# Normalizing and rotating q and k of two token tiles at a time in a hybrid attention layer

## The chip, the cores and the metric

The kernel runs on one core of a Trainium2 chip. The metric is the device time of one launch in microseconds (us), lower is better; a figure is the median of several runs. Engines are named as the profile names them: PE is TensorE (PEld its weight loads), DVE VectorE, ACT ScalarE, POOL GpSimd, SP the engine that issues most DMAs.

## The reference, cut to what matters

One layer of an encoder, 1024 tokens by 1024 channels, float32. The change touches how q and k are made from the normalized input h:

```python
proj = h @ w_in[l]
qa, ka, va, qb, kb, vb, gates = jnp.split(proj, split_at, axis=-1)
qa = rms_norm(qa.reshape(b, s, NA_HEADS, HEAD_DIM), g_qa[l])        # 8 heads of 64, no rotation
ka = rms_norm(ka.reshape(b, s, NA_HEADS, HEAD_DIM), g_ka[l])
o_a = neighbourhood_attention(qa, ka, va, rpb[l])
qb = partial_rotary(rms_norm(qb.reshape(b, s, DIL_HEADS, HEAD_DIM), g_qb[l]), pos)   # 12 heads of 64
kb = partial_rotary(rms_norm(kb.reshape(b, s, DIL_HEADS, HEAD_DIM), g_kb[l]), pos)
# three groups of 4 heads, each with dilated_window_attention; then gates, output projection, SwiGLU FFN
```

`rms_norm` divides each head's 64 values by the root of their mean square plus 1e-6. `partial_rotary` turns the first 16 of the 64 values by an angle that depends on the token.

## The kernel before, in words

The heads are worked in ten units of two heads: units 0 to 5 are the dilated heads (kinds 0, 1 and 2, two units each), units 6 to 9 the neighbourhood heads (the fourth kind, `U.kind == 3`). A unit has eight token tiles of 128 tokens. One step of the main loop, n = 8u + t, multiplies token tile t of unit u: `proj_chunk` (L333) makes 24 matmuls of 384 columns (q, k and v of two heads) into a bank of PSUM with the tag `d`, of which there are two, so that tile t + 2 needs the bank of tile t. Every float32 product is three products of split parts.

After the eight chunks of a step, `proj_post` takes the bank. ACT squares q and k into `sq` (L351) and copies them into `qn` (L352, 128 x 256: two heads of q, two of k). DVE sums the squares (L354), and `rstd` makes 1/rms: a logarithm and an exponential on ACT (L140, L142), then one Newton step on DVE with four small operations of 128 x 4 (L141, L143, L144, L145). DVE multiplies `qn` by it (L356). For kinds 0 to 2 POOL then rotates with four operations (L363 to L366). ACT copies v out (L368 or L371).

Two steps later `qk_turns` (L403) turns `qn` on PE with one transposition for q and one for k of each tile, and `qk_parts` (L425 to L428) writes the split parts into the unit's q and k. Before step 58 (`PAIRED`) the turns are made in odd steps n, for the tiles of steps n - 3 and n - 2 together; in steps 8 and 9 the first four tiles of unit 0 are turned, in steps 11 and 13 its last four. From step 58 each step turns the one tile of step n - 2. Between chunk 4 and chunk 5 of a step stand the scores of an earlier unit, its products with v, the turns, and the transpositions of its probabilities, in that order on PE. Other work of these steps runs on the same engines: the conditioning row `acc` on DVE (L322), weight splits (ACT L129; the low part on DVE or POOL, L130), parts of later weights (`tp`, `w1m`).

The order on PE is written out by hand. The orders on DVE, ACT, POOL and SP in the main loop are made when the program is built, by a list scheduler with a timeline of its own; `proj_post` has a raised priority. Each of these queues runs in order. `qn` has seven buffers of 256 values, taken in turn: the first for a placeholder, the second for the table of cosines, then one for each token tile. Steps up to 81 project and turn; from step 80 the gate matmuls (L773) follow, then merge, output projection and the feed-forward part (L1353, L1418, L1588).

Of the kernel before, what the change touches and what calls it, by code (L numbers as in the profile page):

```python
# [10 lines left out]
F32 = mybir.dt.float32  # L11
F32R = mybir.dt.float32r
AF = mybir.ActivationFunctionType
ALU = mybir.AluOpType
# [7 lines left out]
EPS = 1e-6  # L22
# [19 lines left out]
PAIRED, RBT, COMB = 58, 5, 68  # L42
# [6 lines left out]
def hybrid_layer(ctx: ExitStack, tc: tile.TileContext, x, colp, wada1, wada2, bada2, wqkv, wg, wpa, wpb,  # L49
                 wo, w1, w2, hgain, ropeg, rope, rbias, bmask, g2r, out):  # L50
    nc = tc.nc
# [45 lines left out]
    eps = const.tile([128, 1], F32, name="eps")  # L97
    nc.vector.memset(eps, EPS)
    for i in (0, 2):
        nc.vector.scalar_tensor_tensor(hg[:, i:i + 1], hg[:, i:i + 1], 0.125, hg[:, i + 1:i + 2],  # L100
                                       op0=ALU.mult, op1=ALU.mult)
# [34 lines left out]
    def rstd(p, n, width, ss, tag):  # L136
        v = p.tile([128, width], F32, tag="rv", bufs=3, name="rv")
        y = p.tile([128, width], F32, tag="ry", bufs=3, name="ry")
        z = p.tile([128, width], F32, tag="rz", bufs=3, name="rz")
        nc.scalar.activation(y, ss, AF.Ln, scale=1.0 / n, bias=eps)  # L140
        nc.vector.tensor_scalar(v, ss, 1.0 / n, EPS, op0=ALU.mult, op1=ALU.add)  # L141
        nc.scalar.activation(y, y, AF.Exp, scale=-0.5)  # L142
        nc.vector.tensor_mul(z, y, v)  # L143
        nc.vector.scalar_tensor_tensor(z, z, -0.5, y, op0=ALU.mult, op1=ALU.mult)  # L144
        nc.vector.scalar_tensor_tensor(y, z, 1.5, y, op0=ALU.add, op1=ALU.mult)  # L145
        return y
# [7 lines left out]
    ap_ = pool("attn", "right")  # L154
# [9 lines left out]

    yT = [ap_.tile([128, 4, S], F32, tag="qk", bufs=2, name="yT") for _ in range(2)]
    land = [big("land") for _ in range(NLAND)]
    for tag, n, bufs in (("bm", 512, 1), ("p", 512, 4), ("qn", 256, 7), ("rtab", 512, 1), ("acc2", 512, 1), ("pT", 512, 4),
                         ("stg", 512, 3), ("vs", 128, 2), ("ra", 64, 2), ("rb", 64, 2)):
        ap_.tile([128, n], F32, tag=tag, bufs=bufs, name="place")
    seq = [0]  # L170

# [89 lines left out]
    rtab = []  # L261

    def rope_tab():
        cs = ap_.tile([128, 4, 64], F32, tag="qn", bufs=7, name="cs").rearrange("p h (a b) -> p (h a) b", b=32)
        nc.sync.dma_start(cs, rope)
        tb = ap_.tile([128, 8, 2, 2, 16], F32, tag="rtab", bufs=1, name="rtab")
        for qk in range(2):
            for f in range(2):
                nc.gpsimd.tensor_tensor(tb[:, :, f, qk, :], cs[:, :, f * 16:f * 16 + 16],
                                        rg[:, qk, f, None, :].to_broadcast([128, 8, 16]), op=ALU.mult)  # L270
        return tb

# [71 lines left out]
    @urgent(PP)  # L344
    def proj_post(U, t):
        pd = U.pd[t]
        qn = ap_.tile([128, 4, 64], F32, tag="qn", bufs=7, name="qn")
        U.qn[t] = qn
        pq = pd[:, :256].rearrange("p (h d) -> p h d", h=4)
        sq = ap_.tile([128, 256], F32, tag="sq", bufs=1, name="sq")  # L350
        nc.scalar.activation(sq, pd[:, :256], AF.Square)  # L351
        nc.scalar.activation(qn, pq, AF.Copy)  # L352
        ss = ap_.tile([128, 4], F32, tag="ss4", bufs=2, name="ss4")
        nc.vector.tensor_reduce(ss, sq.rearrange("p (h d) -> p h d", h=4), axis=mybir.AxisListType.X, op=ALU.add)  # L354
        r = rstd(ap_, 64, 4, ss, "q")
        nc.vector.tensor_tensor(qn, qn, r[:, :, None].to_broadcast([128, 4, 64]), op=ALU.mult)  # L356
        if U.kind < 3:
            ra = ap_.tile([128, 4, 16], F32, tag="ra", bufs=2, name="ra")
            rb = ap_.tile([128, 4, 16], F32, tag="rb", bufs=2, name="rb")
            tb = U.tab[:, t]  # L360
            v4 = lambda z: z.rearrange("p (a b) c -> p a b c", a=2)
            tv = lambda f, c0, c1: tb[:, f, :, None, c0:c1].to_broadcast([128, 2, 2, c1 - c0])
            nc.gpsimd.tensor_tensor(v4(ra), v4(qn[:, :, 0:16]), tv(0, 0, 16), op=ALU.mult)  # L363
            nc.gpsimd.tensor_tensor(v4(rb[:, :, 0:8]), v4(qn[:, :, 8:16]), tv(1, 0, 8), op=ALU.mult)
            nc.gpsimd.tensor_tensor(v4(rb[:, :, 8:16]), v4(qn[:, :, 0:8]), tv(1, 8, 16), op=ALU.mult)
            nc.gpsimd.tensor_tensor(qn[:, :, 0:16], ra, rb, op=ALU.add)  # L366
        if U.kind == 0:
            nc.scalar.activation(U.v[:, t, :], pd[:, 256:384], AF.Copy)  # L368
        else:
            vs = ap_.tile([128, 128], F32, tag="vs", bufs=2, name="vs")  # L370
            nc.scalar.activation(vs, pd[:, 256:384], AF.Copy)  # L371
            vd = v_d[U.u - 2]
            if U.kind == 3:
                nc.scalar.dma_start(vd.rearrange("(c r j) d -> r j c d", c=8, r=16)[2 * t:2 * t + 2], vs)
            else:
                nc.scalar.dma_start(vd[t * 128:(t + 1) * 128, :], vs)
            if t == 7:
                U.v = big("v", [128, 8, 128])
# [479 lines left out]
    units = []  # L858
# [147 lines left out]
    for n in range(6, 92):  # L1006
# [46 lines left out]

        turns = [(units[0], tt) for tt in {8: (0, 1), 9: (2, 3), 11: (4, 5), 13: (6, 7)}.get(n, ())]
        if PAIRED <= n <= 81 or 9 < n < PAIRED and n % 2:
            turns += [(units[m // 8], m % 8) for m in ((n - 2,) if n >= PAIRED else (n - 3, n - 2)) if m >= 8]
        chunk()
        chunk()
        if n == PAIRED - 1:
# [693 lines left out]
```

## Time and profile before

| | |
|---|---|
| median of 3 runs | 1496.59 us (1496.54 to 1497.46) |
| the profiled execution: its time / its span from first to last instruction | 1494.47 us / 1492.7 us |
| busy share: PE, DVE, ACT, POOL | 99%, 72%, 47%, 40% |
| mean granted TensorE clock | 0.998 of full speed |

Read the shares with care: matmuls are pipelined and their ends are modelled, so a busy PE is not PE at its peak. Idle time of an engine that is not the bottleneck costs nothing.

### The profile page before, as it was taken

How to read it: one execution, taken by the hardware profiler on the slowest of the kernel's cores; microseconds unless marked ns; L12 is line 12 of the kernel's file. 1: busy time of each engine (PE TensorE's matmuls, PEld its weight loads, DVE VectorE, ACT ScalarE, POOL GpSimd, SP SyncE). 2: the span in 40 equal slices, each digit the busy share in tenths (PEclk: the TensorE clock that was granted, in tenths of full speed). 3: DMA queues.
4: the chain of work that ended last, by engine and by line, in shares of the span. 5: the costliest groups of instructions: out<-in, count | busy, mean ns of one | idle time of the engine just before them, and what ended most of it. 6: DMA issues, size and time to landing. Idle time of an engine off the chain costs nothing. (4 is left out here: it accounts for less than half of the span.)

```text
span 1492.7 us, 24300 instructions
## 1 busy us (share of the span) xinstructions
PE 1473.4 (99%) x8168; PEld 1260.0 (84%) x8168; DVE 1074.1 (72%) x2202; ACT 700.4 (47%) x1775; POOL 591.9 (40%) x580
## 2 busy tenths in 40 slices
PE   9999999999999989999999999999999999999998
PEld 7999998989898867888888888888888888887886
DVE  6877767667768854485765596888777777598468
ACT  5655665556776655465422353323223333354442
POOL 0342342242100122256431402677777775204464
PEclk9999999999999999999999999999999999999999
DMA  9725454576144454773452335345533334898342
GB/s 357 263 73 166 155 164 146 181 243 204 56 138 136 154 198 150 265 291 116 133 192 85 99 92 184 123 144 167 177 106 106 109 107 151 282 369 280 99 155 99
DMA packets 156908, 250.54 MB, mean 168 GB/s; under 512 B 26832, under 2 KB 70512, under 8 KB 156016
## 3 DMA queue, kind: packets, MB, share of 16 engines
q1 hardware_dynamic: 138208, 235.35, 47.0%
q10 hardware_dynamic: 18576, 13.64, 2.8%
q8 instruction: 65, 1.06, 0.3%
q14 instruction: 59, 0.48, 0.1%
HBM read 184.06 MB, written 64.86 MB: 167 GB/s over the span
## 5 line engine op out<-in xcount | busy, mean ns | idle before, releaser
L333 PE MATMUL ps_d<-whi,hT 128*128 128x384 f32 x1152 | 310.2, 340 | 1.6 <-ACT vs L371 0.8
L129 ACT ACTIVATE whi<-raw 128x512 fp32r<-128x512 f32 (+2 forms) x314 | 182.6, 594 | 210.7 <-PE ps_t L1588 33.5
L130 POOL TENSOR_TENSOR wlo<-raw,whi 128x512 fp32r<-128x512 f32 (+2 forms) x123 | 159.9, 1307 | 288.2 <-ACT whi L129 251.9
L130 DVE TENSOR_TENSOR wlo<-raw,whi 128x512 fp32r<-128x512 f32 (+1 forms) x191 | 167.9, 894 | 62.3 <-ACT whi L129 57.0
L333 PEld LDWEIGHTS ps_d<-whi,hT 128*128 128x128 f32 x1152 | 209.2, 188 | 3.6 <-ACT vs L371 1.2
L333 PE MATMUL ps_d<-wlo,hT 128*128 128x384 f32 x576 | 193.0, 335 | 0.8 <-POOL wlo L130 0.6
L333 PEld LDWEIGHTS ps_d<-wlo,hT 128*128 128x128 f32 x576 | 108.4, 188 | 1.3 <-POOL wlo L130 1.3
L129 ACT ACTIVATE whi<-ws 128x512 fp32r<-128x512 f32 x60 | 37.7, 628 | 119.5 <-DVE ws L1435 85.2
L1368 POOL TENSOR_TENSOR e<-e,c 128x512 f32<-128x512 f32 x44 | 68.5, 1556 | 60.6 <-DVE c L1498 36.5
L773 PE MATMUL ps_d<-hT,whi 128*128 128x512 f32 x256 | 81.4, 399 | 3.4 <-ACT whi L129 3.4
L363 POOL TENSOR_TENSOR ra<-qn,rtab 128x64 f32<-128x64 f32 x48 | 17.6, 367 | 142.8 <-DVE qn L356 121.0
L130 POOL TENSOR_TENSOR wlo<-m,whi 128x512 fp32r<-128x512 f32 x35 | 51.9, 1493 | 53.6 <-ACT whi L129 53.6
L1366 ACT ACTIVATE e<-e 128x512 f32<-128x512 f32 x44 | 27.4, 630 | 89.2 <-DVE e L1501 60.7
L130 POOL TENSOR_TENSOR wlo<-gl,whi 128x512 fp32r<-128x512 f32 x26 | 35.4, 1377 | 73.2 <-ACT whi L129 73.2
L581 ACT ACTIVATE P<-P,st 128x256 f32<-128x256 f32 (+2 forms) x100 | 45.7, 458 | 34.1 <-DVE st L579 33.9
L1418 PE MATMUL ps_v<-h2T,whi 128*128 128x512 f32 x192 | 59.2, 390 | 0.0
L1418 PE MATMUL ps_s<-h2T,whi 128*128 128x512 f32 x192 | 59.1, 389 | 0.0
L773 PEld LDWEIGHTS ps_d<-hT,whi 128*128 128x128 f32 x256 | 47.9, 191 | 13.1 <-ACT whi L129 3.6
L1418 PE MATMUL ps_d<-h2T,whi 128*128 128x512 f32 x184 | 56.7, 390 | 0.0
L1367 DVE TENSOR_TENSOR e<-e 128x512 f32<-128x512 f32 x44 | 42.9, 981 | 17.9 <-ACT e L1366 17.8
L140 ACT ACTIVATE ry<-ss,eps 128x4 f32<-128x4 f32 (+1 forms) x88 | 26.2, 298 | 61.1 <-DVE ss L354 45.1
L517 ACT ACTIVATE P<-P,sx 128x384 f32<-128x384 f32 (+1 forms) x64 | 37.2, 582 | 34.3 <-DVE sx L516 34.1
(411 smaller groups left out, 4052.5 us busy)
## 6 DMA issues: line engine op xcount, KB each, us to landing
raw<-in_w_dram SPq DMA_DIRECT2D x139, 256.0 KB, 3.2
ga_d<-e SPq DMA_DIRECT2D x77, 256.0 KB, 2.0
raw<-ga_d SPq DMA_DIRECT2D x77, 256.0 KB, 2.6
wa<-in_wada_dram SPq DMA_DIRECT2D x32, 512.0 KB, 5.3
raw<-in_wqkv_dram SPq DMA_DIRECT2D x80, 192.0 KB, 4.9
m<-in_w_dram SPq DMA_DIRECT2D x44, 256.0 KB, 5.1
xt<-in_x_dram SPq DMA_DIRECT2D x16, 512.0 KB, 4.2
land<-in_wada_dram SPq DMA_DIRECT2D x16, 512.0 KB, 9.3
```

Of the source, the lines that this page charges most:

```text
L129: nc.scalar.activation(hi[:, :n], r, AF.Copy)
L130: (eng or nc.gpsimd).tensor_sub(lo[:, :n], r, fview(hi[:, :n]))
L140: nc.scalar.activation(y, ss, AF.Ln, scale=1.0 / n, bias=eps)
L333: nc.tensor.matmul(pd[:, :384], tok(a, k, t), U.w[k][b][:, :384], start=(k == 0 and i == 0), stop=(k == KT - 1 and i == 2))
L363: nc.gpsimd.tensor_tensor(v4(ra), v4(qn[:, :, 0:16]), tv(0, 0, 16), op=ALU.mult)
L517: nc.scalar.activation(P[:nq, :nk], P[:nq, :nk], AF.Exp, scale=-1.0, bias=nm, accum_out=sm)
L581: nc.scalar.activation(C.P[h][:nq, c], C.P[h][:nq, c], AF.Exp, scale=-1.0, bias=nm, accum_out=sm)
L773: nc.tensor.matmul(pb, w[x][:, k * 128:(k + 1) * 128], b[y][:, k], start=(k == 0 and q == 0), stop=(k == 3 and q == 2))
L1366: nc.scalar.activation(sg, a, AF.Sigmoid)
L1367: nc.vector.tensor_mul(sg, sg, a)
L1368: nc.gpsimd.tensor_mul(sg, sg, up)
L1418: nc.tensor.matmul(pb, w[p][:, k * 128:(k + 1) * 128], b[q][:, k], start=(k == 0 and i == 0), stop=(k == 3 and i == 2))
```

## The change

1. `qn` becomes a tile for two neighbouring token tiles (128 x 8 x 64; three buffers in place of seven of half that size). Each tile still has its own square, copy, sum and copy of v; the copy of v (`proj_v`) stands ahead of the rest.
2. After the odd tile, 1/rms, the multiplication and the rotation are made once for both tiles, at twice the width.
3. The Newton step has two DVE operations in place of four: the copy out of PSUM carries a factor -1/128, ACT squares the estimate, and the constants are folded.
4. The rotation table's axes are reordered to fit, and the small tiles `ra`, `rb` are twice as wide.
5. From step 58 a step turns the tile of step n - 3 in place of n - 2; at t = 1 it turns tiles 6 and 7 of the unit before together, at t = 2 none.

```diff
-                         ("stg", 512, 3), ("vs", 128, 2), ("ra", 64, 2), ("rb", 64, 2)):
+    ... ("qn", 512, 3) for ("qn", 256, 7)
+                         ("stg", 512, 3), ("vs", 128, 2), ("ra", 128, 2), ("rb", 128, 2)):
...
     def proj_post(U, t):
         pd = U.pd[t]
-        qn = ap_.tile([128, 4, 64], F32, tag="qn", bufs=7, name="qn")
-        U.qn[t] = qn
+        i = t % 2
+        if i == 0:
+            U.two = (ap_.tile([128, 8, 64], F32, tag="qn", bufs=3, name="qn"),
+                     ap_.tile([128, 8], F32, tag="ss4", bufs=2, name="ss4"))
+        qn, ss = U.two
+        hs = slice(4 * i, 4 * i + 4)
+        U.qn[t] = qn[:, hs]
...
-        nc.scalar.activation(qn, pq, AF.Copy)
-        ss = ap_.tile([128, 4], F32, tag="ss4", bufs=2, name="ss4")
-        nc.vector.tensor_reduce(ss, sq.rearrange("p (h d) -> p h d", h=4), axis=mybir.AxisListType.X, op=ALU.add)
-        r = rstd(ap_, 64, 4, ss, "q")
-        nc.vector.tensor_tensor(qn, qn, r[:, :, None].to_broadcast([128, 4, 64]), op=ALU.mult)
+        nc.scalar.activation(qn[:, hs], pq, AF.Copy, scale=-1.0 / 128)
+        nc.vector.tensor_reduce(ss[:, hs], sq.rearrange("p (h d) -> p h d", h=4), axis=mybir.AxisListType.X, op=ALU.add)
+        proj_v(U, t, pd)
+        if i == 0:
+            return
+        y, y2, z, r = (ap_.tile([128, 8], F32, tag=g, bufs=3, name=g) for g in ("rv", "ry", "rz", "rz"))
+        nc.scalar.activation(y, ss, AF.Ln, scale=1.0 / 64, bias=eps)
+        nc.scalar.activation(y, y, AF.Exp, scale=-0.5)
+        nc.scalar.activation(y2, y, AF.Square)
+        nc.vector.scalar_tensor_tensor(z, ss, 64 * EPS, y2, op0=ALU.add, op1=ALU.mult)
+        nc.vector.scalar_tensor_tensor(r, z, -192.0, y, op0=ALU.add, op1=ALU.mult)
+        nc.vector.tensor_tensor(qn, qn, r[:, :, None].to_broadcast([128, 8, 64]), op=ALU.mult)
         if U.kind < 3:
...
+            nc.gpsimd.tensor_tensor(...)  four rotation operations, each over [128, 8, 16] or [128, 8, 8]
...
-            turns += [(units[m // 8], m % 8) for m in ((n - 2,) if n >= PAIRED else (n - 3, n - 2)) if m >= 8]
+            turns += [(units[m // 8], m % 8) for m in ((n - 3, n - 2)[:(2, 0)[t - 1] if t in (1, 2) else 1] if n >= PAIRED else (n - 3, n - 2)) if m >= 8]
```

## Rows read from the trace of the kernel before

**Rows 1.** The page's first part: busy us, share of the span, instructions.
```profile
PE 1473.4 (99%) x8168; PEld 1260.0 (84%) x8168; DVE 1074.1 (72%) x2202; ACT 700.4 (47%) x1775; POOL 591.9 (40%) x580
```
**Rows 2.** Busy time by stretch: us, each engine's busy us (instructions), clock, DMA.
```profile
90.00:320.00 230.00, 225.92 (x1694) 211.20 (x1693) 163.76 (x542) 136.83 (x480) 73.42 (x174) 1.00 0.48 153
320.00:520.00 200.00, 199.16 (x1459) 179.12 (x1457) 154.01 (x526) 137.34 (x453) 29.88 (x25) 1.00 0.48 154
520.00:550.00 30.00, 25.55 (x149) 19.21 (x149) 16.96 (x39) 14.81 (x39) 9.12 (x7) 0.94 0.62 208
550.00:1300.00 750.00, 750.00 (x3436) 619.54 (x3435) 523.60 (x706) 282.46 (x528) 377.59 (x264) 1.00 0.45 152
```
**Rows 3.** PE's waits from 50 to 560: us in total, times, longest.
```profile
PE ps_v L403 <- POOL qn L366: 2.7, 3, 1.3
...
PE ps_d L333 <- ACT vs L371: 0.8, 1, 0.8
PE ps_d L333 <- ACT whi L129: 0.8, 1, 0.8
PE ps_d L333 <- POOL wlo L130: 0.6, 1, 0.6
```
**Rows 4.** DVE groups from 56 to 520, shapes apart: busy us, mean ns, idle before.
```profile
L356 DVE TENSOR_TENSOR qn<-qn,ry 128x256 f32<-128x256 f32 x80 | 36.6, 458 | 3.0
...
L143 DVE TENSOR_TENSOR rz<-ry,rv 128x4 f32<-128x4 f32 x80 | 25.8, 322 | 29.1 <-ACT ry L142 28.4
...
L141 DVE TENSOR_SCALAR rv<-ss 128x4 f32<-128x4 f32 x80 | 17.1, 214 | 1.5
L145 DVE SCALAR_TENSOR_TENSOR ry<-rz,ry 128x4 f32<-128x4 f32 x80 | 14.2, 178 | 1.3
...
L144 DVE SCALAR_TENSOR_TENSOR rz<-rz,ry 128x4 f32<-128x4 f32 x80 | 13.3, 166 | 1.8
...
L827 DVE TENSOR_TENSOR tp<-tp 128x512 f32<-128x512 f32 x8 | 5.6, 704 | 6.7 <-DMA tp<-h_d 6.6
```
**Rows 5.** ACT groups from 56 to 520, shapes apart.
```profile
L140 ACT ACTIVATE ry<-ss,eps 128x4 f32<-128x4 f32 x80 | 23.9, 298 | 59.8 <-DVE ss L354 45.1 <-DVE rv L141 8.0 <-DMA raw<-in_wqkv_dram 2.9
...
L142 ACT ACTIVATE ry<-ry 128x4 f32<-128x4 f32 x80 | 16.2, 203 | 1.7
```
**Rows 6.** POOL groups from 56 to 520, shapes apart.
```profile
L363 POOL TENSOR_TENSOR ra<-qn,rtab 128x64 f32<-128x64 f32 x48 | 17.6, 367 | 142.8 <-DVE qn L356 121.0 <-DVE rv L141 13.3 <-DVE rz L143 7.6
...
L364 POOL TENSOR_TENSOR rb<-qn,rtab 128x32 f32<-128x32 f32 x48 | 14.4, 300 | 0.0
```
**Rows 7.** PE at 143 to 145: start us, us, instruction, idle before.
```profile
144.31 0.44 PE L403 MATMUL ps_v<-ident,qn 128*128 128x128 f32 x2 [0.24 <-POOL qn L366]
```
**Rows 8.** PE at 189 to 197.
```profile
193.21 0.44 PE L403 MATMUL ps_v<-ident,qn 128*128 128x128 f32 x2 [1.16 <-POOL qn L366]
```
**Rows 9.** PE at 303 to 305.
```profile
304.24 0.44 PE L403 MATMUL ps_v<-ident,qn 128*128 128x128 f32 x2 [1.28 <-POOL qn L366]
```
**Rows 10.** PE at 276 to 279: four transpositions in one row.
```profile
277.81 0.83 PE L403 MATMUL ps_v<-ident,qn 128*128 128x128 f32 x4
```
**Rows 11.** PE at 130 to 133.
```profile
131.91 0.66 PE L403 MATMUL ps_v<-ident,qn 128*128 128x128 f32 x4
```
**Rows 12.** POOL at 185 to 194.
```profile
186.48 1.37 POOL L363 TENSOR_TENSOR ra<-qn,rtab 128x64 f32<-128x64 f32 x1 [7.54 <-DVE qn L356]
187.81 1.71 POOL L364 TENSOR_TENSOR rb<-qn,rtab 128x32 f32<-128x32 f32 x1
```
**Rows 13.** PE at 78 to 79, the end of step 9 and the start of step 10.
```profile
77.93 0.60 PE L403 MATMUL ps_s<-ident,qn 128*128 128x128 f32 x4
78.29 0.42 PE L333 MATMUL ps_d<-whi,hT 128*128 128x384 f32 x1
```
**Rows 14.** ACT at 73 to 75.
```profile
73.88 0.38 ACT L352 ACTIVATE qn<-ps_t 128x256 f32<-128x256 f32 x1
```

More of the change, by code (lines that the diff above doesn't have):

```diff
@@ L166, in hybrid_layer @@
     land = [big("land") for _ in range(NLAND)]
-    for tag, n, bufs in (("bm", 512, 1), ("p", 512, 4), ("qn", 256, 7), ("rtab", 512, 1), ("acc2", 512, 1), ("pT", 512, 4),
-                         ("stg", 512, 3), ("vs", 128, 2), ("ra", 64, 2), ("rb", 64, 2)):
+    for tag, n, bufs in (("bm", 512, 1), ("p", 512, 4), ("qn", 512, 3), ("rtab", 512, 1), ("acc2", 512, 1), ("pT", 512, 4),
+                         ("stg", 512, 3), ("vs", 128, 2), ("ra", 128, 2), ("rb", 128, 2)):
         ap_.tile([128, n], F32, tag=tag, bufs=bufs, name="place")
@@ L263, in rope_tab @@
     def rope_tab():
-        cs = ap_.tile([128, 4, 64], F32, tag="qn", bufs=7, name="cs").rearrange("p h (a b) -> p (h a) b", b=32)
+        cs = ap_.tile([128, 8, 64], F32, tag="qn", bufs=3, name="cs")[:, :4].rearrange("p h (a b) -> p (h a) b", b=32)
         nc.sync.dma_start(cs, rope)
-        tb = ap_.tile([128, 8, 2, 2, 16], F32, tag="rtab", bufs=1, name="rtab")
+        tb = ap_.tile([128, 2, 8, 2, 16], F32, tag="rtab", bufs=1, name="rtab")
         for qk in range(2):
             for f in range(2):
-                nc.gpsimd.tensor_tensor(tb[:, :, f, qk, :], cs[:, :, f * 16:f * 16 + 16],
+                nc.gpsimd.tensor_tensor(tb[:, f, :, qk, :], cs[:, :, f * 16:f * 16 + 16],
                                         rg[:, qk, f, None, :].to_broadcast([128, 8, 16]), op=ALU.mult)
@@ L351, in proj_post @@
         nc.scalar.activation(sq, pd[:, :256], AF.Square)
-        nc.scalar.activation(qn, pq, AF.Copy)
-        ss = ap_.tile([128, 4], F32, tag="ss4", bufs=2, name="ss4")
-        nc.vector.tensor_reduce(ss, sq.rearrange("p (h d) -> p h d", h=4), axis=mybir.AxisListType.X, op=ALU.add)
-        r = rstd(ap_, 64, 4, ss, "q")
-        nc.vector.tensor_tensor(qn, qn, r[:, :, None].to_broadcast([128, 4, 64]), op=ALU.mult)
-        if U.kind < 3:
[L358 to L362, printed above, removed]
+        nc.scalar.activation(qn[:, hs], pq, AF.Copy, scale=-1.0 / 128)
[10 more added lines that the diff above has]
+        nc.vector.tensor_tensor(qn, qn, r[:, :, None].to_broadcast([128, 8, 64]), op=ALU.mult)
+        if U.kind < 3:
+            ra = ap_.tile([128, 8, 16], F32, tag="ra", bufs=2, name="ra")
+            rb = ap_.tile([128, 8, 16], F32, tag="rb", bufs=2, name="rb")
+            tb = U.tab[:, :, t - 1:t + 1].rearrange("p f t a c -> p f (t a) c")
+            v4 = lambda z: z.rearrange("p (a b) c -> p a b c", b=2)
+            tv = lambda f, c0, c1: tb[:, f, :, None, c0:c1].to_broadcast([128, 4, 2, c1 - c0])
             nc.gpsimd.tensor_tensor(v4(ra), v4(qn[:, :, 0:16]), tv(0, 0, 16), op=ALU.mult)
@@ L366, in proj_post, with proj_v @@
             nc.gpsimd.tensor_tensor(qn[:, :, 0:16], ra, rb, op=ALU.add)
+    def proj_v(U, t, pd):
         if U.kind == 0:
```

## The prediction

> **What bounds the kernel now.** I read the page's first part first, then busy time by stretch, then PE's waits, then the operations that the change touches, then single stretches of the timeline. The first part shows PE busy for 1473.4 of 1492.7 us [rows 1]; all its idle time is 19.3 us, and whatever the other engines save can only come out of that. The stretches show where it lies: 4.08 us between 90 and 320 (kinds 0 to 2), 0.84 between 320 and 520 (the fourth kind), 4.45 between 520 and 550, and none from 550 to 1300 [rows 2]. The rest lies in the start and the tail, which the change does not touch.
>
> PE's waits in the projection steps say what could be won: three waits at the turns, L403, for POOL's last rotation operation, 2.7 us together; one for a bank that ACT had not yet copied out, 0.8; one for a high weight part on ACT, 0.8; one for a low part on POOL, 0.6 [rows 3]. Together 4.9 us, a third of a per cent. A change of under 0.2%, 3 us, can hardly be told from none on this kernel. The idle time between 520 and 550 stands at the gates' weights, after the last unit; the change moves no load and no gate operation there, so I leave it.
>
> **The change part by part.** The sum is made on the profiled execution, 1494.47 us, with 1492.7 of span and 1.8 around it; it stands 2.1 under the median of the runs, 1496.59.
>
> *What DVE and ACT get rid of.* Each of 80 tiles costs DVE L141, L143, L144, L145 and L356, 0.214 + 0.322 + 0.166 + 0.178 + 0.458 = 1.338 us, 107 us in all [rows 4]. After the change each of 40 pairs has two small operations like L144 and L145 and one multiplication of 128 x 512. That one is not in the trace; the nearest row is L827, a two-operand operation of that size, 0.704 [rows 4]. So 40 x (0.166 + 0.178 + 0.704) = 42 us, 65 us less. ACT loses 80 x (0.298 + 0.203) = 40 us for the logarithm and the exponential and gets back half of it, and 40 squares of 128 x 8, which I bound by these two operations, 0.2 to 0.3 us [rows 5]: some 10 us less. None of this counts by itself: between 90 and 320 DVE is busy 163.76 of 230 us and PE 225.92 [rows 2], and PE's matmuls hide it. It counts where it shortens a queue that PE waits for.
>
> *The chain of the odd tile grows.* Until now the even tile was finished a step ahead; now the odd tile's chain does it for both. The multiplication grows by 0.704 - 0.458 = 0.25 us. On POOL an operation of 64 values takes 0.367 and one of 32 takes 0.300 [rows 6], two of each for a tile: 1.33 us. The slope is 0.067 for 32 values, so 128 values give about 0.50, and the pair 2 x (0.50 + 0.367) = 1.74, 0.40 more. (Bounds: no growth, and twice, 1.33 more.) The Newton step loses L143, 0.322, and gets the square, 0.2 to 0.3: nearly nothing. So the pair is ready 0.25 + 0.40 - 0.07 = about 0.58 us later after the same start in kinds 0 to 2, 0.2 in the fourth.
>
> *What this meets at the turns.* Before step 58 the turn comes in the second step after the odd tile's projection, before and after the change. Three turns already wait, at 144.31, 193.21 and 304.24 [rows 7 to 9], and one at 277.81 takes 0.83 us for its four transpositions, where an undisturbed one takes 0.66 [rows 10, 11]: it has no slack either. With the queues as they stand, these four end 4 x 0.58 = 2.3 us later, and at the three that wait the even tile's two transpositions, 0.22 each time by the pitch of the rows, no longer run ahead: 0.66. Together +3.0. The other end: DVE no longer works off the even tile's chain and one link less stands in the odd one's, so that less foreign work gets in between, and all 2.7 us of waiting go. The queue orders are made anew when the program is built, so the trace cannot say which; I take the middle, +0.1, and keep both ends.
>
> *The other waits.* The copy of v now stands ahead of 1/rms, and ACT, DVE and POOL have less to do. The bank wait and the two weight waits, 0.8 + 0.8 + 0.6 [rows 3], may go, all or none; as a new order can make others of their kind, I take off less than half, 0.9.
>
> *Three buffers for seven.* In steady state a `qn` tile is turned at least a step before its buffer is wanted again. Not at the start. The placeholder, the cosine table and the pairs take buffers in turn, so tiles 0 and 1 of unit 1 get the buffer of tiles 2 and 3 of unit 0, which are turned at the end of step 9. The copy of unit 1's tile 0, now made right after step 8, must wait for that, and it holds bank `d`, which the first matmul of step 10 wants. That matmul follows the four transpositions directly: they start at 77.93 and end at 78.53, the matmul starts at 78.29 [rows 13]. A copy takes 0.38 [rows 14], so the bank is free at 78.91 at the earliest: 0.62 us of new waiting, 1.0 if one more copy stands ahead. I take 0.7. Behind that copy ACT's queue holds this step's other copies, for which nobody waits before step 11.
>
> *The fourth kind a step later.* From a tile's being ready to its turn it is two steps now; it stays two for the even tiles and for 6 and 7, and becomes three for the other odd ones. Scores need all eight tiles, and tiles 6 and 7 are still turned at t = 1, one step ahead of the first scores. Three units lose one turn each, a handful of ACT and DVE operations under a PE that idles 0.84 us in that whole stretch [rows 2]. I count nothing; without that cover it would be 0.4 us per operation, on ACT or DVE alone. No DMA is added, and none of SP's moves past another.
>
> *Sum:* +0.1 - 0.9 + 0.7 = -0.1 us: 1494.4 for a profiled execution, 1496.5 for the median.
>
> **The rivals.** *Faster: the stalls go.* All 4.9 us of the projection steps' waits vanish and the bank wait of step 10 stays: -4.2, 1492.4. For it: DVE has 65 us less in stretches where it is busy seven tenths, and each of the waits was a queue that ran late, not a lack of throughput. Against it: the three longest end on POOL, whose chain grows.
>
> *Slower: rotation of the pair gets stretched by VectorE.* At 186.48 one rotation operation took 1.37 us and the next 1.71, four to six times their usual length, [rows 12] against [rows 6]. If POOL's two longer operations of the pair meet such a neighbour, the pair is late by more. It decides from 0.58 us at the four tight turns on, with nothing won back (+3.0 + 0.7). At 1.0 us: 4 x 1.0 + 0.66 + 0.7 = +5.4, 1502.0 without the relief, 1501.1 with it. For it: such stretches exist. Against it: their means, 0.367 and 0.300, hold them already.
> The Trainium skill, GPSIMD Engine Reference, section 8 (Key points), says that this engine shares its SBUF interfaces with VectorE and contends with VectorE instructions that have two SBUF inputs; the stretched rows agree with it, as such operations run beside them, and the pair's multiplication is one more of that sort, twice as long. By it the change would go against itself; the price is the one above.
>
> *The change does nothing at all for PE:* all waits stay as they are but for step 10's, +0.7, 1497.3. That is inside "no change" as well.
>
> **How the numbers follow.** No measurable change: 0.52, as the whole stake on either side is about 5 us and the terms have both signs. Faster by over 3 us: 0.24; nearly all of the waits must go. Slower by over 3 us: 0.24; the pair must be late at several turns. The likeliest case by itself reaches from 1493.6 to 1499.6. The range takes in all waits won, 1496.6 - 5.1, and a pair that is a microsecond late, 1501.5.
>
> **What would show it.** Right: PE's idle time between 90 and 320 stays at 2 to 6 us; the multiplication takes about 0.7 us and POOL's two wide operations about 0.5; PE waits 0.6 to 1.0 us for ACT near 78; DVE's busy time falls by some 65 us and the total does not follow. Wrong: turns that wait for POOL in most units, a new wait of the fourth kind's scores, or a changed stretch between 520 and 550, where the clock was 0.94 [rows 2] behind a stall; a stall that moves there would cost or give back more than its own length.

## The result and the profile after

The changed kernel takes 1503.38 us (median of 4 runs, 1502.5 to 1505.48), the kernel before 1496.70 beside it (1496.54 to 1497.46): 1.0045 times as long, 95% interval 1.003 to 1.006, or 6.7 us. The forecast said 1496.5 and 1491.5 to 1501.5. It is slower, beyond the range. The profiled execution took 1503.9, span 1502.1.

The page's first part of the changed kernel answers to [rows 1]:

```profile
PE 1475.9 (98%) x8168; PEld 1261.7 (84%) x8168; DVE 1029.0 (69%) x1916; ACT 693.6 (46%) x1729; POOL 573.3 (38%) x484
```

VectorE (DVE) works 45 us less (the times of its single operations, added up, fall by 61; the records overlap, and busy time counts an overlap once), ScalarE (ACT) 7, POOL 19; PE's idle time went from 19.3 to 26.2 us. Work was saved, and PE waits more. The stretches of the changed kernel answer to [rows 2]:

```profile
90.00:320.00 230.00, 225.52 (x1683) 211.37 (x1682) 144.32 (x410) 134.78 (x468) 56.13 (x100) 0.99 0.45 144
320.00:520.00 200.00, 196.56 (x1442) 178.65 (x1441) 133.83 (x404) 131.37 (x426) 31.97 (x27) 1.00 0.48 157
520.00:550.00 30.00, 25.23 (x154) 18.67 (x153) 17.74 (x45) 14.27 (x39) 2.58 (x2) 0.92 0.62 214
550.00:1300.00 750.00, 750.00 (x3441) 618.77 (x3440) 519.42 (x709) 284.85 (x535) 384.42 (x268) 1.00 0.45 149
```

From 90 to 320 PE idles 4.48 us (before 4.08), which looks like nothing; from 320 to 520 it idles 3.44 (before 0.84). PE's waits from 50 to 560 answer to [rows 3] (total, times, longest):

```profile
PE ps_d L787 <- ACT whi L129: 4.4, 1, 4.4
PE ps_v L417 <- POOL qn L378: 2.6, 4, 1.2
PE ps_d L333 <- POOL wlo L130: 2.1, 2, 1.4
PE ps_s L516 <- DVE qk L442: 1.8, 1, 1.8
PE ps_v L417 <- DVE qn L368: 1.3, 1, 1.3
PE ps_d L333 <- ACT whi L129: 1.3, 1, 1.3
PE ps_d L333 <- ACT v L382: 0.7, 1, 0.7
PE ps_s L516 <- ACT qk L440: 0.3, 1, 0.3
```

L787 stands at the gates and is no part of the change. The other lines sum to 10.1 us where [rows 3] had 4.9. New are the fourth kind's scores L516 (2.1), a turn that waits for VectorE's multiplication (1.3; at 332.62 in step 51, the first pair of unit 6, so a turn of the fourth kind, which has no rotation), a bank that waits for the copy of v (0.7, at step 10) and one more wait for a low weight part (1.4). The new operations on VectorE and POOL from 56 to 520 answer to [rows 4] and [rows 6]:

```profile
L368 DVE TENSOR_TENSOR qn<-qn,rz 128x512 f32<-128x512 f32 x39 | 27.0, 692 | 3.0 <-ACT qn L357 0.6 <-DVE rz L367 0.5
L366 DVE SCALAR_TENSOR_TENSOR rz<-ss,ry 128x8 f32<-128x8 f32 x39 | 10.0, 257 | 24.5 <-ACT ry L365 24.5
L367 DVE SCALAR_TENSOR_TENSOR rz<-rz,rv 128x8 f32<-128x8 f32 x39 | 8.2, 209 | 0.9
```

```profile
L378 POOL TENSOR_TENSOR qn<-ra,rb 128x128 f32<-128x128 f32 x24 | 12.7, 529 | 1.6
L375 POOL TENSOR_TENSOR ra<-qn,rtab 128x128 f32<-128x128 f32 x24 | 12.1, 505 | 156.8 <-DVE qn L368 116.1 <-ACT sq L356 13.1 <-DVE rz L367 11.5
L376 POOL TENSOR_TENSOR rb<-qn,rtab 128x64 f32<-128x64 f32 x24 | 10.2, 423 | 0.0
L377 POOL TENSOR_TENSOR rb<-qn,rtab 128x64 f32<-128x64 f32 x24 | 9.5, 398 | 0.0
```

A pair's rotation is 1.855 us long (forecast 1.74).

**Where the time went.** PE runs the same 8168 matmuls before and after, so the start of the k-th can be compared in the two traces. The difference grows by 9.4 us in all, since this profiled execution of before was a short one (1494.47). It grows by 1.3 before 56 us, where nothing was changed; executions differ by that much (`e2` below, as little changed there, is 0.8 ahead at 38 us). Then come 1.31 at 74.87 (low part), 0.92 at 81.8 (bank), 2.0 up to 269 (0.4 of it in the weights' wait that ends at 263.39, 1.6 behind it), 1.33 at 272.4 (turn), 1.33 at 332.6 (turn), 2.4 at 421.9 to 424.1 (scores), and 1.3 at the gates. Some places come out better: turns of the rotated kinds by 1.33 at 196.5 and 1.56 at 309, and by 1.21 at 339.4 a bank for which PE waited before [rows 3]. Over the rotated kinds' own turns the differences nearly cancel.

**The scores at 424.** The timeline of the changed kernel around them, only the operations of this turn and what stands ahead of them:

```profile
416.13 0.66 PE L417 MATMUL ps_v<-ident,qn 128*128 128x128 f32 x4
...
418.30 0.75 DVE L322 SCALAR_TENSOR_TENSOR acc<-wa,cact,acc 128x512 f32<-128x512 f32 x1 [2.00 <-DMA wa<-in_wada_dram]
...
419.42 0.51 ACT L531 ACTIVATE P<-P,sx 128x256 f32<-128x256 f32 x1 [2.08 <-DVE sx L530]
...
420.70 0.69 ACT L439 ACTIVATE qk<-ps_v,hg 128x256 fp32r<-128x256 f32 x1
...
421.19 0.65 ACT L440 ACTIVATE qk<-ps_v 128x256 fp32r<-128x256 f32 x1
...
421.44 1.54 DVE L322 SCALAR_TENSOR_TENSOR acc<-wa,cact,acc 128x512 f32<-128x512 f32 x2 [0.79 <-DMA wa<-in_wada_dram]
...
422.90 0.64 DVE L441 SCALAR_TENSOR_TENSOR qk<-ps_v,hg,qk 128x256 fp32r<-128x256 f32 x1
...
423.44 0.58 DVE L442 TENSOR_TENSOR qk<-ps_v,qk 128x256 fp32r<-128x256 f32 x1
...
424.08 0.50 PE L516 MATMUL ps_s<-qk 64*128 64x256 f32 x4 [1.80 <-DVE qk L442]
```

The same place in the kernel before:

```profile
411.32 0.44 PE L403 MATMUL ps_v<-ident,qn 128*128 128x128 f32 x2
...
413.59 0.47 ACT L425 ACTIVATE qk<-ps_v,hg 128x128 fp32r<-128x128 f32 x1
...
415.66 0.44 DVE L427 SCALAR_TENSOR_TENSOR qk<-ps_v,hg,qk 128x128 fp32r<-128x128 f32 x1
...
416.02 0.38 DVE L428 TENSOR_TENSOR qk<-ps_v,qk 128x128 fp32r<-128x128 f32 x1
...
416.51 0.63 PE L502 MATMUL ps_s<-qk 64*128 64x256 f32 x6
```

Before, one tile is turned in the step ahead of the scores: ScalarE begins to evict it 2.3 us after the start of the transpositions, and VectorE is done at 416.40, 0.11 us before the scores start. There was no slack at this place, the first scores of unit 7. (At those of unit 8 VectorE was done 3.2 us ahead, at 468.86 for 472.05; after the change it ends 0.4 us behind the scores' start, at 479.69 for 479.33, and PE loses under 0.3 us.) Now two tiles are turned in that step. The evictions are twice as wide (0.69 and 0.65 on ScalarE for 0.47, 0.64 and 0.58 on VectorE for 0.44 and 0.38), and ScalarE begins them 4.6 us after the start of the transpositions, behind exponentials that wait for VectorE, which itself waits for a load of the ada weights.

### The profile page after: what moved, and what is told of

It is laid out like the page before. It is cut to its first block, busy times and chain, and to the rows that moved or that the text cites. A ratio compares the mean times of both kernels' runs of the same rounds, so it can differ in the third digit from the quotient of the medians.

```text
span 1502.1 us, 23816 instructions
## 1 busy us (share of the span) xinstructions
PE 1475.9 (98%) x8168; PEld 1261.7 (84%) x8168; DVE 1029.0 (69%) x1916; ACT 693.6 (46%) x1729; POOL 573.3 (38%) x484
## 4 chain that ended last, share of the span: by engine, by line
PE 80%; DMA 7%; DVE 6%; ACT 3%; issue 2%; POOL 1%; SPq 1%; ACTq 0%; DVEq 0%; POOLq 0%
PE ps_d L333 13%; PE ps_v L1432 7%; PE ps_d L1432 7%; PE ps_s L1432 7%; PE ps_t L1432 6%; PE ps_d L787 5%; PE ps_s L1602 3%; PE ps_d L1602 3%; PE ps_s L1367 2%; PE ps_d L1367 2%; PE ps_v L1602 2%; PE ps_t L1602 2%; DVE wlo L130 2%; PE ps_v L1367 1%; PE ps_v L1218 1%
## 5 line engine op out<-in xcount | busy, mean ns | idle before, releaser
L787 PE MATMUL ps_d<-hT,whi 128*128 128x512 f32 x256 | 82.3, 403 | 4.4 <-ACT whi L129 4.4
L375 POOL TENSOR_TENSOR ra<-qn,rtab 128x128 f32<-128x128 f32 x24 | 12.1, 505 | 156.8 <-DVE qn L368 116.1
L787 PEld LDWEIGHTS ps_d<-hT,whi 128*128 128x128 f32 x256 | 48.4, 193 | 14.3 <-ACT whi L129 4.7
L358 DVE TENSOR_REDUCE ss<-sq 128x4 f32<-128x256 f32 x80 | 33.2, 414 | 32.0 <-ACT sq L356 31.9
```

What stands on the lines that cost most here:

```text
L358: nc.vector.tensor_reduce(ss[:, hs], sq.rearrange("p (h d) -> p h d", h=4), axis=mybir.AxisListType.X, op=ALU.add)
L787: nc.tensor.matmul(pb, w[x][:, k * 128:(k + 1) * 128], b[y][:, k], start=(k == 0 and q == 0), stop=(k == 3 and q == 2))
```

## The experiments

Theory Q: evictions and normalizations stand in the new queue orders behind operations that wait for loads. Rival L: the pair's longer chain costs. Rival N: any new queue order costs. Rival W, added later: two tiles turned in the step just ahead of the scores. P and V, later still, are explained where they come. All ratios are against the kernel before on the same chip, with 95% intervals. The waits of a kernel come from one execution, which took between 2.5 us less (`e8`) and 5.0 us more (`e7`) than the median of its runs.

**One part alone, or one undone**

`e1`: the two-operation Newton step per tile, nothing else.

```diff
-        r = rstd(ap_, 64, 4, ss, "q")
+        y, y2, z, r = (ap_.tile([128, 4], ...) ...)   # Ln, Exp, Square, two VectorE operations
```

> The kernel before, with the Newton step of 1/rms in two VectorE operations and a square on ScalarE, for each tile by itself: no pairs, seven buffers, the turns where they were. Theory Q (what was lost lies in where the new queue orders put q and k work behind operations that wait for a DMA, above all at the scores of the fourth kind, which waited 1.80 us for VectorE at 424.08): this edit takes work away and leaves the shape of the chain, so 1494 to 1498 us, with no wait of the first fourth-kind scores of a unit. Rival L (the longer chain and the longer rotation of a pair cost): the same, 1494 to 1498, as there is no pair here. Rival N (any rebuilt order lands some 5 us higher, because the order of before is a lucky one): 1500 to 1504.

1496.15 us, 0.9996 (0.9987 to 1.0004). The Newton step costs nothing and brings nothing; N, that any new queue order is worse, falls. Q and L forecast the same here and are not told apart.

`e2`: the later turn alone.

```diff
-   for m in ((n - 2,) if n >= PAIRED else (n - 3, n - 2))
+   for m in ((n - 3, n - 2)[:(2, 0)[t - 1] if t in (1, 2) else 1] if n >= PAIRED else (n - 3, n - 2))
```

> The kernel before, with only the turns of the fourth kind's odd tiles moved one step later; each tile is still normalized by itself. Theory Q, if the place of the turn is what counts: the two turns at t = 1 put their copies behind VectorE's accumulations that wait for the ada weights, the first scores wait about 1.8 us as they did in the changed kernel, and the time is 1498.5 to 1501. If what counts is that the pair's normalization is late, and not the turn: no new wait at the scores and 1495 to 1498. Rival L: 1495 to 1498. Rival N: 1500 to 1504.

1501.47 us, 1.0034 (1.0022 to 1.0046): 5 us from this one line, which the forecast counted as nothing; just over Q's 1498.5 to 1501, with the wait where Q put it. The line moves more than odd tiles: every tile but 7 turns one step later, and tile 6, which turned at t = 0, now turns at t = 1 together with tile 7. PE's waits in it at the scores (50 to 560):

```profile
PE ps_s L502 <- DVE qk L428: 1.4, 1, 1.4
...
PE ps_s L502 <- ACT qk L426: 1.0, 1, 1.0
```

The 2.4 us are at 418 and 419.8, and there is more behind them: the stretches of this run there (us, busy times, clock next to last but two).

```profile
416.00:420.00 4.00, 1.58 (x10) 1.06 (x10) 3.96 (x10) 2.92 (x10) 0.00 (x0) 0.98 0.89 318
420.00:423.00 3.00, 3.00 (x21) 2.44 (x22) 1.77 (x11) 2.02 (x8) 0.00 (x0) 0.50 0.43 144
```

After 2.42 idle us of 4 the granted clock was 0.50 for the next 3, and the lag grew from 3.0 to 4.7 us while PE waited for nothing: with that the stall cost 1.7 times its length.

`e3`: pairs in the rotated kinds, the fourth kind as before.

```diff
-        if i == 0:
+        if i == 0 and U.kind < 3:
             return
+        if U.kind == 3: qn, ss = qn[:, hs], ss[:, hs]     # and the turn at n - 2
```

> The changed kernel, but in the fourth kind each tile is normalized by itself and turned where the kernel before turned it; pairs are left in the three rotated kinds. Theory Q: the waits of 1.80 and 0.33 us at the fourth kind's first scores go, and perhaps what follows between 520 and 550; 1499 to 1501.5. Rival L: the loss lies in the three rotated kinds, so 1502.5 to 1504. Rival N: 1500 to 1504, with the waits in other places.

1499.91 us, 1.0023 (1.0014 to 1.0033). The scores' waits are gone, and half of the loss with them; the other half lies in the rotated kinds. The time is Q's; as half of the loss stays, both Q and L had a part.

`e4`: the turns' priority raised.

```diff
-PP, QT, AQ, AT, AV = 100, 0, 0, 0, 0
+PP, QT, AQ, AT, AV = 100, 100, 0, 0, 0
```

> The changed kernel, with the turns' copies given the raised priority that the projections' operations already have (one constant, 0 to 100). Theory Q: the scheduler puts the copies ahead of the accumulations that wait for the ada weights, so the scores' wait of 1.80 us goes and the time is 1498 to 1501. Rival L: no change, 1502.5 to 1504, as the chain that the turn waits for is as long as it was. Rival N: 1500 to 1504.

1504.05 us, 1.0042 (1.003 to 1.0054). Q's number missed. The scores' wait fell from 2.1 to 1.0, but turns waited 6.1 us from 90 to 345 in place of 3.9 (4.8 and 2.6 of these in the rotated kinds, 1.3 both times at unit 6's first pair). Priority moves the waits about.

**Is it the loads that VectorE waits for?**

`e5`, `e6`: accumulations on a pair loaded earlier, in the changed kernel and in the kernel before.

```diff
-        wa = ada_acc["w"][i - kk % 2][:, kk % 2, :]
+        wa = ada_acc["w"][max(i - kk % 2 - 2, 0)][:, kk % 2, :]
```

> The changed kernel, but each ada accumulation on VectorE multiplies the weight pair loaded one pair earlier, which has landed long before, so the ada rows are wrong numbers of the right shape; loads, instructions and their count stay. VectorE then has no reason to wait for these loads (8.8 us in six places between 50 and 580 in the changed kernel). Theory Q (q and k evictions stand in VectorE's queue behind accumulations that wait for a load): the scores' wait of 1.80 us at 424.08 and the wait of 1.33 us at 332.6 go, 1499 to 1501 us, which is 1.000 to 1.0025 times the kernel before with the same substitution. Rival W (the turn of two tiles in the step ahead of the scores has twice the evictions, and that alone makes the scores wait): the scores still wait about 1 us, 1501 to 1503. Rival L (the longer chain of a pair): no change, 1502.5 to 1504.

> The kernel before with the same substitution in the ada accumulations (their rows are wrong numbers of the right shape), as the base for the run above. In the kernel before VectorE waits 4.9 us in three places for these loads, while PE idles 0.84 us from 320 to 520. Every theory expects little here: 1493 to 1498 us. If it is faster by over 3 us, the loads' waits cost the kernel before as well.

1.0045 (1.003 to 1.0061) and 1.0021 (1.001 to 1.0032). Q's time missed, and so did the forecast for `e6`, 1493 to 1498: it took 1500.80. The edit did not do its work where it mattered: at 416.15 VectorE still waited 2.42 us for a weight pair that was asked for one pair earlier, and the scores waited 2.5 us. The pair of runs is 0.24% apart in place of 0.45%, within Q's 1.000 to 1.0025 for the two; but as the base moved too, and the wait stayed, I read nothing from it.

`e11`: seven accumulations left out.

```diff
-        else:
+        elif not 46 <= i <= 53:
             nc.vector.scalar_tensor_tensor(ada_acc[c], wa, ...)
```

> The changed kernel without seven of the ada accumulations on VectorE, those of steps 60 to 69 (two of the eight rows of the modulation then come out wrong; their loads stay). It takes away what stands ahead of VectorE's max and sums in the step of the late turn: VectorE idled 2.00 and 0.79 us there for a weight load, ScalarE's exponentials waited for VectorE, and the turn's evictions stood behind these exponentials, 4.2 us after the transpositions. Theory Q (the evictions are late because they stand behind an operation that waits for a load): the scores' wait in unit 7 is under 0.5 us, 1.0025 to 1.004 times the kernel before. Rival W without Q (the doubled evictions are late by their own width): the wait stays over 1 us and the time at 1.004 to 1.005.

1.0044 (1.0029 to 1.0058), with 0.9 us of the scores' wait left. The wait is neither Q's (under 0.5) nor W's (over 1); the time is W's. Another accumulation moved into the gap (at 421.39, after 2.64 us for its load) and stood ahead of VectorE's evictions again. That is Q's mechanism, which neither `e5` nor `e11` took away, so they don't tell Q from W.

**Two tiles in the step ahead of the scores**

`e9`: the kernel before, all turns later as in `e2`, but the double turn at t = 0.

```diff
+   for m in ({0: (n - 3, n - 2), 1: (n - 2,), 2: ()}.get(t, (n - 3,)) if n >= PAIRED else (n - 3, n - 2))
```

> The kernel before, each tile normalized by itself, with the fourth kind's turns one step later as in the run with the later turn alone (which came out 1.0034 times the kernel before), but the last turn of each unit spread otherwise: the step that turns two tiles is t = 0 (tiles 5 and 6), and t = 1, the step ahead of the first scores, turns tile 7 alone as the kernel before does. Theory W (two tiles turned in the step just ahead of the scores have evictions that are twice as wide, and ScalarE's and VectorE's queues take them up too late): no wait at 424 or its like, 0.999 to 1.0015 times the kernel before. Rival (any later turn in the fourth kind costs, wherever it lies): 1.0025 to 1.004.

1496.06 us, 0.9996 (0.9987 to 1.0004), the time that W said: the 5 us of `e2` are gone. The scores' wait there is not quite gone:

```profile
PE ps_s L502 <- DVE qk L428: 0.5, 1, 0.5
```

The trace of `e9` also tells W from Q at this place:

```profile
412.87 0.44 PE L403 MATMUL ps_v<-ident,qn 128*128 128x128 f32 x2
...
415.43 0.75 DVE L322 SCALAR_TENSOR_TENSOR acc<-wa,cact,acc 128x512 f32<-128x512 f32 x1 [2.95 <-DMA wa<-in_wada_dram]
...
417.07 0.47 ACT L425 ACTIVATE qk<-ps_v,hg 128x128 fp32r<-128x128 f32 x1
...
418.96 0.51 PE L502 MATMUL ps_s<-qk 64*128 64x256 f32 x4 [0.52 <-DVE qk L428]
```

VectorE waits 2.95 us for its load and ScalarE begins the eviction 4.2 us after the turn's start, nearly as late as in the changed kernel, and yet the scores wait 0.5 us and not 2.1. VectorE is done 6.0 us after the turn's start with one tile (`e9`), 7.9 with two (the changed kernel; `e2` 8.2). A late load with one tile behind it cost little here. How much of the rest is the evictions' double width, and how much their place in the two queues, is not separated.

The later turns of tiles 0 to 5 are free; tile 6's turn at t = 1, beside tile 7's, is not.

`e10`: the changed kernel with the last pair of each fourth-kind unit apart.

```diff
-        if i == 0:
+        if i == 0 and (U.kind < 3 or t < 6):
             return
+        if U.kind == 3 and t >= 6: qn, ss = qn[:, hs], ss[:, hs]     # and the turns of e9
```

> The changed kernel with one part undone: in the fourth kind tiles 6 and 7 are normalized each by itself, so tile 6 can turn at t = 0 (together with tile 5) and tile 7 alone at t = 1, as in the run above; all other pairs stay. Theory W: the 1.80 us at 424.08 and 0.33 us at its like one unit later go, 1.0045 falls to 1.002 to 1.0035. Rival L (length of the pair's chain in the rotated kinds): 1.004 to 1.0055.

1.0033 (1.002 to 1.0045), and 0.2 us left of the scores' wait. (Both waits of the changed kernel, 0.3 and 1.8, stand in step 66, not one unit apart.) In W's range, though the intervals of this and of the whole change overlap.

**The rotated kinds**

`e7`: the pair rotated tile by tile.

```diff
+            for j in range(2):
+                q = qn[:, 4 * j:4 * j + 4]          # eight operations of half the width
```

> The changed kernel, with the pair normalized together but rotated tile by tile on POOL, with eight operations of half the width for each pair instead of four: by the means of before 2.67 us of rotation for a pair against some 1.7, so each turn of the rotated kinds has 0.9 us more ahead of it. Rival L: the turns that wait for POOL (2.6 us) wait longer and others begin to, +3 to +6 us: 1506 to 1509. Theory Q: what a turn waits for is whatever stands between these operations, not their own length; within 2 us of the changed kernel, 1501.5 to 1505.5.

1.0074 (1.0058 to 1.0091). By the means of its trace a pair's rotation is now 2.65 us, 0.79 longer, and the kernel is some 4 us slower than the changed one. L's mechanism exists, and the time, 1508.15 us, is in its range. PE's waits at the turns from 90 to 345 (this execution took 1513.12 us, 5 over the median; the 2.2 are at unit 6's first pair, where nothing is rotated):

```profile
PE ps_v L419 <- POOL qn L380: 5.6, 7, 1.3
PE ps_v L419 <- DVE qn L368: 2.2, 1, 2.2
```

`e8`: the first unit's tiles 2 and 3 turned a step sooner.

```diff
-   {8: (0, 1), 9: (2, 3), 11: (4, 5), 13: (6, 7)}
+   {8: (0, 1, 2, 3), 11: (4, 5), 13: (6, 7)}
```

> The changed kernel, with the first unit's tiles 2 and 3 turned in step 8 beside tiles 0 and 1, not in step 9, so that their buffer is free before the second unit's first copy wants it. The forecast's term (d), three buffers for seven, was +0.7 us, and the changed kernel showed 0.92 us at 81.8: if it is the buffer, that wait goes and the time is 1502 to 1503. If another operation on ScalarE holds the bank, it stays. If step 8 then waits for the four turns' tiles instead, 1503 to 1505.

The wait at step 10 is gone, and PE starts there 0.83 us sooner against the changed kernel; the time, 1.0047 (1.0034 to 1.0061), misses the 1502 to 1503; it can't show so little, and in this execution another turn waited longer, 2.6 us at 271.0.

`e12`: pairs only in the rotated units behind the first. The text speaks of units 1 to 6; the rotated units are 0 to 5, so these are units 1 to 5.

```diff
+        alone = U.kind == 3 or U.u == 0     # these tile by tile; and the turns of e8
```

> Pairs only in units 1 to 6: the first unit and the fourth kind are normalized and rotated tile by tile (with the two-operation Newton step), the fourth kind turns where the kernel before did, and the first unit's tiles 0 to 3 all turn in step 8. By the ledger of the two traces this leaves out the waits at 74.87 (1.31 us, low weight parts behind POOL's rotation), 81.8 (0.92, bank) and 424 (2.6): if these places hold the loss, 0.999 to 1.0015 times the kernel before. Rival L (each pair's turn costs, everywhere in the rotated kinds): 1.002 to 1.004, with turns that wait for POOL over 5 us together. If it comes out under 0.998 it is the version that beats both.

1.004 (1.0028 to 1.0052): missed. It is L's number, and turns wait 5.5 us for POOL as L had it, but not where L put them: with unpaired tiles the four were not ready in step 8, and one turn waited 2.9 us for POOL at 77.4, with the clock at half behind it; the turns of the later rotated units wait 2.6 as in the changed kernel. An edit that was to take a wait away made a larger one.

`e13`, `e14`: low weight parts of the later units on VectorE, with the change and (beside the Newton step) without it. Theory P: low parts in POOL's queue make the rotation late. Rival V: VectorE's queue takes over.

```diff
-   nextw[u + 1, k] = wsplit(raws[u + 1, k], nc.vector if k % 2 else None)
+   nextw[u + 1, k] = wsplit(raws[u + 1, k], nc.vector)
```

> The changed kernel, with all low weight parts of the later units computed on VectorE, so that in these steps POOL's queue holds little but the rotation. Theory P (a turn is late because a low part stands between the pair's rotation operations and waits for ScalarE's high part, which waits for a load): the turns' waits for POOL, 2.6 us in the changed kernel, fall under 1 and the low parts' wait at 74.87 goes, 1.0045 falls to 1.0015 to 1.003. Rival L (the pair's chain is too long for its step): they stay, 1.004 to 1.005. Rival V (VectorE's queue takes over: turns wait for its multiplication behind the low parts): waits for POOL go and waits for VectorE come, 1.004 to 1.007.

> The kernel before with the two-operation Newton step and the low weight parts of the later units on VectorE, no pairs. Theory P: the turns' waits for POOL, 2.7 us in the kernel before, go: 0.997 to 0.999 times the kernel before, which would beat both. Rival V: 1.000 to 1.003, with turns or weights that wait for VectorE.

1.0022 (1.0009 to 1.0035) and 0.9997 (0.9988 to 1.0006). For `e13` P's number, but not P's reason: turns still wait, 2.9 us for POOL in the rotated kinds and 2.0 for VectorE in the fourth (90 to 345). What went are the waits for the weights, 3.4 us in the changed kernel, 0.2 here, and the half clock behind them; the scores' wait is smaller too, 1.2 for 2.1. `e14` missed P's gain: without pairs the same move brings nothing (`e1` alone has 0.9996).

`e16`, `e18`: the rotation of the pair on VectorE, first with the whole change, then with the fourth kind as before and the turns of `e8`.

```diff
-            nc.gpsimd.tensor_tensor(...)     # four times
+            nc.vector.tensor_tensor(...)
```

> The changed kernel, with the pair's four rotation operations on VectorE, so that nothing of the chain from the projection to the turn runs on POOL and one hand-over less stands in it; VectorE gets some 25 to 35 us more work in the rotated kinds, where it has 144 of 230 us now. Rival L: the chain is shorter, so the turns come earlier: 1.001 to 1.0035. Theory P: POOL's low parts no longer stand in the way either: the same range, with no turn that waits for POOL. Rival V (what stands in VectorE's queue decides): 1.0045 to 1.008.

> Pairs in the six rotated units alone, rotation of the pair on VectorE, the fourth kind as in the kernel before, the first unit's tiles 0 to 3 turned in step 8; the low parts stay where the changed kernel has them. If the pair's chain over POOL is what made the turns late: 0.998 to 1.0005. If VectorE's queue makes them late in its place (with the rest of the change the run with this rotation had 4.7 us of turns that waited for VectorE): 1.001 to 1.0025.

1.0017 (1.0006 to 1.0028) and 0.9993 (0.9984 to 1.0001), in the ranges for a shorter chain. That the turns come earlier is not shown for `e16`: those of the rotated kinds still wait 2.5 us, now for VectorE, and the fourth kind's 2.2; in `e18` it is 1.4 and 1.9. The four operations are 1.10 us there by their means, 1.86 on POOL. The Trainium skill, Trainium Architecture — The Big Picture, The five engines, in one table, has POOL at half of VectorE's speed for streaming elementwise work; here it is 0.6 of it. `e16` still has the scores' wait, 2.3 us.

`e15`, `e17`: all known losses undone. `e15` has pairs in the rotated units only, the turns of `e8` and the low parts of `e13`; `e17` has the whole change with the repairs of `e8`, `e10` and `e13`.

> Pairs in the six rotated units alone, the fourth kind as in the kernel before, the first unit's tiles 0 to 3 turned in step 8, and low weight parts of the later units on VectorE: all that was seen to lose, undone, with the pairs left. Theory P: 0.998 to 1.001. Rival L: 1.0015 to 1.003, as the pairs' turns are late on their own account. Rival V: 1.003 or more.

> The changed kernel with three repairs together: in the fourth kind tiles 6 and 7 normalized each by itself and turned in different steps, the first unit's tiles 0 to 3 turned in step 8, and the low weight parts of the later units on VectorE. If the three places hold the whole loss and pairs as such are free: 0.999 to 1.001 times the kernel before, without a wait of the fourth kind's scores over 0.5 us. Rival (the other pairs of the fourth kind cost by their later turns): 1.0015 to 1.003.

1.0001 (0.9992 to 1.0009) and 0.9993 (0.9983 to 1.0003). PE's waits at turns, scores and weights in `e17`, 50 to 560:

```profile
PE ps_v L421 <- POOL qn L382: 3.7, 4, 1.2
...
PE ps_v L421 <- DVE qn L372: 2.4, 2, 1.6
```

Both are in the range for undone losses. No scores and no weights wait any more in `e17`, and the whole loss is gone. The turns still wait 6.1 us in this execution, which took 1499.36 us, 2.6 over the median of its runs; what makes up for them is not shown. No version beats the kernel before by more than can be measured.

## Why the prediction was wrong

*What bounds the kernel* held: PE, and only its waits count. 45 us less on VectorE (forecast 65) shortened nothing.

*What DVE and ACT get rid of* was sized well (the multiplication 0.692 for a forecast 0.704; the five operations' 107 us became 40 x (0.692 + 0.257 + 0.209) = 46, forecast 42; ACT 7 less, forecast 10), and "none of this counts by itself" was right.

**The step that failed** is *the fourth kind a step later*: "I count nothing". The text says that tiles 6 and 7 are "still" turned at t = 1, one step ahead of the first scores. That holds for tile 7 alone: before, tile 6 was turned at t = 0, so the change puts a second tile into the step ahead of the scores. And the text argued from PE's idle time in the whole stretch, 0.84 us in 200, that there is cover, and did not look at how long before the scores the last eviction ends. At unit 7 it was 0.11 us, with one tile; with two the scores waited 2.1 us. `e2` measures this step by itself at 1.0034, 5 us; `e9` shows that the second tile in that step is the cause, and not the later turns or the late loads alone. Undone inside the whole change it gives back less, 1.0045 to 1.0033 (`e10`) or to 1.0023 with the fourth kind's pairs (`e3`): the parts don't add up exactly.

*The other waits*, -0.9, had the wrong sign: weights waited 3.4 us where they had waited 1.4 [rows 3], while the bank wait of 0.8 did go. `e13` takes the weights' waits away, and part of the scores', and comes out at 1.0022. The low part that PE waited for at 74.87 stood behind the rotation of two pairs, from 66.58 on, in which three of the four narrow operations took 0.77 to 0.79 us beside VectorE's work, where their mean is 0.41:

```profile
67.00 0.77 POOL L376 TENSOR_TENSOR rb<-qn,rtab 128x64 f32<-128x64 f32 x1
67.73 0.77 POOL L377 TENSOR_TENSOR rb<-qn,rtab 128x64 f32<-128x64 f32 x1
68.47 1.33 POOL L130 TENSOR_TENSOR wlo<-raw,whi 128x384 fp32r<-128x384 f32 x1
...
73.08 0.79 POOL L377 TENSOR_TENSOR rb<-qn,rtab 128x64 f32<-128x64 f32 x1
```

*The chain of the odd tile*, +0.1, came out at +1.2 in these two executions, but not where the text looked. The growth itself was right (0.23 us on VectorE, 0.50 on POOL). From 90 to 345 turns wait 3.9 us in the changed kernel, 2.7 before; 1.3 of the 3.9 is unit 6's first pair, and in the rotated kinds it is 2.6, no more than before. Over the kernels with pairs rotated on POOL in four operations (all but `e7`, `e16` and `e18` of those with pairs) the rotated kinds' turns wait 2.6 to 4.9 us there, over those without 1.3 to 3.6, so pairs tend to wait longer, though each figure is one execution. What the working left out is what else stands in POOL's queue between the pair's operations. The timeline of the longest wait for POOL in the changed kernel shows how a late load gets into the chain:

```profile
270.32 0.53 ACT L129 ACTIVATE whi<-raw 128x384 fp32r<-128x384 f32 x1 [2.44 <-DMA raw<-in_wqkv_dram]
...
270.93 1.00 POOL L130 TENSOR_TENSOR wlo<-raw,whi 128x384 fp32r<-128x384 f32 x1 [1.27 <-ACT whi L129]
...
271.89 0.45 POOL L378 TENSOR_TENSOR qn<-ra,rb 128x128 f32<-128x128 f32 x1
...
272.39 0.33 PE L417 MATMUL ps_v<-ident,qn 128*128 128x128 f32 x1 [1.22 <-POOL qn L378]
```

The pair's last rotation operation stands behind a low part, this behind the high part on ScalarE, and this behind a load. Whether a shorter chain alone would help stays open: `e7` lengthens it and loses, but in `e13` and `e17` the turns wait as long as ever while the time falls.

The half of the loss that lies in the rotated kinds (`e3`, 1.0023) ends with either of two edits: the low parts moved from POOL to VectorE (`e15`, 1.0001), or the rotation moved there (`e18`, 0.9993). Both have the turns of `e8` too, which alone brought nothing, and without pairs moving the low parts brings nothing either (`e14`). The reading that fits all of these is that the pair's rotation and the low parts cost where they share one queue; that two rebuilt orders fell well by luck is not excluded. In both, the rotated kinds' turns wait less than in `e3` (2.6 and 1.4 us for 3.9) and so do the weights (0.9 and 1.4 for 2.6); in `e13` beside the changed kernel only the weights do. Through which of the two it costs more stays open.

*Three buffers for seven* was right: 0.70 us of wait at step 10, forecast 0.62 to 1.0, and `e8` removes it.

*The rivals.* The slower one had the right side and nearly the time, 1501.1 to 1502.0, but gave the loss to stretched rotation alone, while half of it lies in the fourth kind, which has none. Stretched rotation is a part of it at 74.87, as the Trainium skill's GPSIMD Engine Reference, section 8 (Key points), would have it, but in the mean a pair's rotation was only 0.12 us over the forecast. Among the signs of being wrong the text did list a new wait of the fourth kind's scores; it had no price and no chance. Two readings were off: of the three longest waits of the kernel before, two end on POOL (1.28 and 1.16 us), the third is the bank's 0.8; and the pair's multiplication is twice as wide as a tile's but, at 0.704 for 0.458, 1.5 times as long.

## What to carry to other kernels

Before calling a moved step free, look in the trace for the last operation that its consumer waits for and read how long before the consumer it ends, at every place where the step occurs (here 0.11 us at one unit and 3.2 at the next); the stretch's idle time doesn't tell. Joining work of two tiles saves operations but makes the consumer wait for both, so keep the last pair before a consumer apart. When an engine that isn't the bottleneck gets 45 us less to do and nothing comes of it, count what its queue order does to the waits, not its busy time. Where one queue holds two kinds of work that PE waits for, try moving either away.

## What the hardware showed unexpectedly

The granted clock fell to 0.50, the lower of its two levels, some time behind a stall, and not behind each: in `e2` after 2.42 idle us of 4 it was 0.50 for 3 us, while in the changed kernel 1.72 idle us of 2 before 424 left it at 1.00 up to 426. The changed kernel's stretches around the weights' wait at 263.39 show a late drop:

```profile
262.00:264.00 2.00, 0.56 (x2) 0.19 (x1) 0.81 (x3) 2.00 (x7) 0.59 (x1) 1.00 0.00 0
264.00:266.00 2.00, 1.54 (x8) 1.54 (x9) 2.00 (x4) 0.46 (x3) 0.41 (x1) 0.88 0.11 33
266.00:268.00 2.00, 2.00 (x8) 2.00 (x7) 1.12 (x6) 1.43 (x6) 0.00 (x0) 0.50 0.55 196
```

From 263.39 to 269.17 the same matmuls took 5.78 us that took 4.22 before (259.66 to 263.88), with PE busy throughout the last three.

VectorE's operations with two inputs took longer while POOL worked beside them. In the changed kernel, from 56 to 520, its low parts of 128 x 384 took 0.55 us in the mean where POOL did nothing at the time (4 of them) and 0.96 where it did (23), its accumulations 0.75 (42) and 1.01 (14). In `e13`, with 43 low parts taken from POOL, VectorE spent 38.2 us on 70 of them, where it had spent 24.6 on 28:

```profile
L130 DVE TENSOR_TENSOR wlo<-raw,whi 128x384 fp32r<-128x384 f32 x70 | 38.2, 580 | 12.8 <-ACT whi L129 12.3
```
